# A hybrid GLA and NSA decoder trunk on one core: off-diagonal probability blocks of two head groups in fp32

## The chip, the cores and the metric

The kernel runs on one NeuronCore of a Trainium2 chip. The metric is the device time of one execution in microseconds; what is compared is the median of several runs. The core has five engines that matter here: TensorE (PE in the profile, its weight loads are PEld), VectorE (DVE), ScalarE (ACT), GpSimd (POOL) and SyncE (SP), which issues DMAs.

## The reference

The kernel computes two layers on 512 tokens of 1024 channels: a gated linear attention (GLA) and a native sparse attention (NSA), each followed by a mixture of 16 experts, with a layer norm behind every part. The change lies in the NSA. With 512 tokens in blocks of 64 there are 8 blocks and the selection takes up to 16, so all causal blocks are selected, and the window of 512 reaches back over all tokens. What remains are three causal softmax attentions per head, mixed by sigmoid gates:

```python
p_cmp = masked_softmax(einsum(q, k_cmp), cmask);  o_cmp = p_cmp @ v_cmp
p_slc = masked_softmax(einsum(q, k_sel), smask);  o_slc = p_slc @ v_sel
p_win = masked_softmax(einsum(q, k_win), wmask);  o_win = p_win @ v_win
o = gate0 * o_cmp + gate1 * o_slc + gate2 * o_win
```

There are 16 heads in 4 groups; a group shares keys and values.

## The kernel before

Most products are made of fp16 halves: a value is split into a high part (a cast) and a low part (the value less the high part), and high x high, high x low and low x high are accumulated.

The attention is `nsa_attn` (line 1405). Its unit of work is (t, g, b): token tile t of 128 queries, head group g of 4 heads, and branch b (0 selected, 1 window). `order` (lines 1507 and 1508) has 32 units: i = 0 to 7 are tile 3, i = 8 to 15 tile 2 (for g = 0: i = 8 and 9, for g = 1: i = 10 and 11), i = 16 to 23 tile 1, i = 24 to 31 tile 0. `begin(i + 2)` starts the scores of a unit two units ahead of its `pv`.

`scores` (1443) goes over the key tiles j from t down to 0. Two matmuls of 512 columns make a bank of transposed scores for four heads (1448, 1449); the exponential (1452) reads it. A block whose `exact` is set has its exponential written as fp32 into the tile `ph`; that holds for the diagonal block j == t of tiles 2, 1 and 0 (1450), which GpSimd masks (1455). Any other block has it written into a buffer `pf`, of which there are three, and `split` (1411) makes the halves in `ph`. Which engine makes the high half goes by a running count through `HI_BY = 'daeeee'`: d is a VectorE cast, a a ScalarE copy, e a second exponential on ScalarE straight from the bank (where the block was masked, a copy). The low half is a subtraction on VectorE, or, for tile 3 alone, at times on GpSimd.

`pv` (1461) multiplies, per head: for a diagonal block of tiles 2 to 0 one fp32 product with `VF`, the fp32 copy of V (1469), for any other block three narrow fp16 products with the halves of V (1472 to 1474). `V` and `VF` carry a column of ones, so the sum for the softmax comes with the 64 values: 65 columns. `combine` (1489) takes the reciprocal of that sum, multiplies by the gate, and adds into the row `o` (1493 to 1505). `cmp_pv` (1477) does the compressed branch with matmuls on 32 rows (1483 to 1486).

There are eight PSUM banks for all of it. The attention is interleaved with other work: the output projection's weight units are split in i = 5, 6, 8 and 11 (`whl` from `wha`, lines 178 and 180); behind tile 3's last unit come its transposes (273), and from i = 11 its output projection (256 to 258). The order of the instructions on an engine is set when the program is built, by dependence and by their order in the source; an engine then works through its own queue in order.

Of the kernel before, what the change touches and what calls it, by code (L numbers as in the profile page):

```python
# [9 lines left out]
F32 = mybir.dt.float32  # L10
# [11 lines left out]
NT = 4  # L22
# [20 lines left out]
OTT = 1  # L43
REST_AT = (0, 2, 3, 4)
CMP_AT = 4
SPLIT_AT = (5, 6, 8, 11)
SPLIT_BY = 'dddd'
WCH = 4
# [11 lines left out]
class Trunk:  # L60
# [1344 lines left out]
    def nsa_attn(self, T, pool, early, rest, kcA, kcB, vc, kA, kB, V, VF, qA, qB, gate):  # L1405
        nc = self.nc
# [4 lines left out]
        def split(hi, lo, src, ps=None, share=False):  # L1411
            i = cnt[0]
            cnt[0] += 1
            how = HI_BY[i % len(HI_BY)]
            if how == "e" and ps is not None:
                self.exp_ins = nc.scalar.activation(hi, ps, AF.Exp)
            elif how in "ea":
                nc.scalar.activation(hi, src, AF.Copy)
            else:
                nc.vector.tensor_copy(hi, src)  # L1420
            if share and ps is not None and LO_BY[i % len(LO_BY)] == "p":
                nc.gpsimd.tensor_sub(lo, src, hi)
            else:
                nc.vector.tensor_sub(lo, src, hi)

        def cmp_scores(t):
            cs = self.bank()
            nc.tensor.matmul(cs.rearrange("p (h q) -> p h q", h=4), self.identb,
                             self.cmt[:, t][:, None, :].to_broadcast([P, 4, P]), start=True, stop=False,
                             skip_group_check=True)  # L1430
            for g in range(4):
                gs = slice(g * 32, (g + 1) * 32)
                nc.tensor.matmul(cs[gs], kcA[:, gs], qa(g, t), start=False, stop=False, skip_group_check=True,
                                 tile_position=(0, g * 32))
                nc.tensor.matmul(cs[gs], kcB[:70, gs], qb(g, t), start=False, stop=(g == 3), skip_group_check=True,
                                 tile_position=(0, g * 32))
            pc = T([P, S], "pf", F32, 3)
            nc.scalar.activation(pc, cs, AF.Exp)
            pch = T([P, 2, S], "pch", F16, 2)
            split(pch[:, 0], pch[:, 1], pc)  # L1440
            return pch

        def scores(t, g, b):
            ph = self.wp.tile([P, 4, 2, S], F16, name="ph", tag="wst", bufs=NST)
            for j in range(t, -1, -1):
                st = self.bank()
                js = slice(j * P, (j + 1) * P)
                nc.tensor.matmul(st, kA[b][:, g, js], qa(g, t), start=True, stop=False)
                nc.tensor.matmul(st, kB[b][:70, g, js], qb(g, t), start=False, stop=True)
                exact = j == t < NT - 1  # L1450
                pf = ph[:, j].rearrange("p i q -> p (i q)").bitcast(F32) if exact else T([P, S], "pf", F32, 3)
                self.exp_ins = nc.scalar.activation(pf, st, AF.Exp)
                if j == t:
                    v = pf.rearrange("p (h q) -> p h q", h=4)
                    nc.gpsimd.affine_select(v, v, pattern=[[0, 4], [1, P]], compare_op=OP.is_ge, fill=0.0,
                                            base=0, channel_multiplier=-1)
                if not exact:
                    split(ph[:, j, 0], ph[:, j, 1], pf, None if j == t else st, t == NT - 1)
            return ph

        def pv(t, g, b, ph):
            ob = self.bank()
            for h in range(4):
                hs = slice(h * P, (h + 1) * P)
                o0 = ob[:, h * 65:(h + 1) * 65]
                exact = t < NT - 1
                if exact:
                    pf = ph[:, t].rearrange("p i q -> p (i q)").bitcast(F32)
                    nc.tensor.matmul(o0, pf[:, hs], VF[b][t][:, g], start=True, stop=(t == 0))
                last = t if exact else t + 1  # L1470
                for j in range(last):
                    nc.tensor.matmul(o0, ph[:, j, 0, hs], V[b][j][:, g, 0:65], start=(j == 0 and not exact), stop=False)
                    nc.tensor.matmul(o0[:, :64], ph[:, j, 0, hs], V[b][j][:, g, 65:129], start=False, stop=False)
                    nc.tensor.matmul(o0, ph[:, j, 1, hs], V[b][j][:, g, 0:65], start=False, stop=(j == last - 1))
            return ob

        def cmp_pv(g, pch):
# [31 lines left out]
        pch, o, ph = {}, {}, {}  # L1509

        def begin(i):
            if i < len(order):
                t, g, b = order[i]
                if g == 0 and b == 0:
                    if t < 3:
                        pch[t] = cmp_scores(t)
                    o[t] = self.row("o")
                ph[i] = scores(t, g, b)
# [4 lines left out]
        for i, (t, g, b) in enumerate(order):  # L1523
# [5 lines left out]
            if t < 3 and b == 0:  # L1529
                combine(t, g, 0, cmp_pv(g, pch[t]), o[t], True)  # L1530
            combine(t, g, 1 + b, pv(t, g, b, ph.pop(i)), o[t], t == 3 and b == 0)
            self.pump()
            if i == REST_AT[-1]:
# [7 lines left out]
                units = [self.fetch_aside(u) for u in range(3)]  # L1541
            if i in SPLIT_AT:
                by = SPLIT_BY[SPLIT_AT.index(i)]
                self.op[0].append(self.split(units.pop(0), (), nc.gpsimd if by == "p" else None))
                if i == SPLIT_AT[0]:
                    units.append(self.fetch_aside(3))
            if i == CMP_AT:
                pch[3] = cmp_scores(3)
# [133 lines left out]
```

## Time and profile before

| | us |
|---|---|
| median of three runs (954.68 to 956.17) | 954.74 |
| profiled execution | 952.24 |
| its span, first to last instruction | 950.5 |
| TensorE busy | 877.9 |
| VectorE busy | 744.7 |
| ScalarE busy | 555.7 |
| GpSimd busy | 310.8 |

The attention takes the stretch from about 575 to 725 us of the span. In the rows below a line gives the start or the stretch first, then a duration; L1472 is line 1472 of the kernel, `bank<-V,ph` what is written and read, a bracket behind it the idle time of the engine just before it and what ended it. TensorE's matmuls overlap, so the pace of a run of them is read from start to start.

### The profile page before, as it was taken

What the parts mean: (1) busy time and instruction counts of PE and PEld (TensorE: products, weight loads), DVE (VectorE), ACT (ScalarE), POOL (GpSimd) and SP (SyncE); (2) the same over time, 40 slices, a digit from 0 to 9 for tenths busy, and PEclk for the clock granted to TensorE, in tenths of its full rate; (3) what the DMA queues carried; (4) which work ended last, traced back from release to release, by engine and by line L of the source; (5) the groups of instructions that cost most, each with busy time, mean ns of one, the idle gap of its engine ahead of it and who ended that gap; (6) DMA issues with size and microseconds to landing.
All of it is one profiled execution on the core that took longest, in us unless ns stands there. A gap on an engine that the chain in (4) does not pass through costs nothing. (4 is left out here: it accounts for less than half of the span.)

```text
span 950.5 us, 26582 instructions
## 1 busy us (share of the span) xinstructions
PE 877.9 (92%) x11218; PEld 718.4 (76%) x11218; DVE 744.7 (78%) x1666; ACT 555.7 (58%) x1174; POOL 310.8 (33%) x349
## 2 busy tenths in 40 slices
PE   6999999996799999899989998999999669999994
PEld 2468888876698989668978885767888568888871
DVE  5972225889899999798678765689777899999967
ACT  4823324424499999724644437784544449999940
POOL 0210021003435241530254524543430348623153
PEclk9999999998899999999999999979999879999997
DMA  8662322072399998871322001120005549999683
GB/s 294 247 205 84 128 90 89 1 300 86 114 374 408 377 378 314 212 205 46 134 89 90 1 3 45 52 85 1 2 2 225 219 180 384 404 369 378 238 156 111
DMA packets 29278, 169.19 MB, mean 178 GB/s; under 512 B 3521, under 2 KB 4161, under 8 KB 12641
## 3 DMA queue, kind: packets, MB, share of 16 engines
q1 hardware_dynamic: 23168, 144.49, 40.0%
q0 software_dynamic: 3072, 12.72, 6.0%
q10 hardware_dynamic: 2912, 10.23, 2.8%
q8 instruction: 90, 1.47, 0.6%
q14 instruction: 36, 0.29, 0.1%
HBM read 153.91 MB, written 13.50 MB: 176 GB/s over the span
## 5 line engine op out<-in xcount | busy, mean ns | idle before, releaser
L834 POOL TENSOR_SCALAR ohe<-icap,rt_px 128x96 f16<-128x96 f32 x112 | 114.1, 1033 | 132.8 <-PE bank L923 124.4
L180 DVE SCALAR_TENSOR_TENSOR whl<-wsu,whl 128x512 f16<-128x512 f32 x192 | 127.2, 714 | 2.9 <-ACT whl L178 2.8
L180 DVE SCALAR_TENSOR_TENSOR whl<-wst,whl 128x512 f16<-128x512 f32 x116 | 75.5, 702 | 67.4 <-ACT whl L178 67.4
L178 ACT ACTIVATE whl<-wsu 128x512 f16<-128x512 f32 x192 | 106.7, 624 | 3.2 <-PE bank L258 3.2
L845 PE MATMUL bank<-ohe,xs 128*128 128x96 f16 x2048 | 99.1, 212 | 6.6 <-DVE ohe L834 5.5
L178 ACT ACTIVATE whl<-wst 128x512 f16<-128x512 f32 x144 | 80.8, 624 | 33.1 <-PE bank L249 9.8
L845 PEld LDWEIGHTS <-xs 128*128 128x128 f16 x2048 | 94.5, 101 | 7.2 <-DVE ohe L834 4.5
L180 DVE SCALAR_TENSOR_TENSOR wha<-wst,wha 128x512 f16<-128x512 f32 x144 | 94.1, 705 | 3.1 <-ACT wha L178 3.0
L258 PE MATMUL bank<-whl,xt 128*128 128x256 f16 x320 | 87.1, 273 | 1.0 <-DVE xt L232 1.0
L256 PE MATMUL bank<-whl,xt 128*128 128x256 f16 x320 | 87.2, 273 | 0.8 <-ACT xt L231 0.7
L257 PE MATMUL bank<-whl,xt 128*128 128x256 f16 x320 | 87.2, 273 | 0.0
L178 ACT ACTIVATE wha<-wst 128x512 f16<-128x512 f32 x144 | 79.8, 623 | 3.4 <-DMA wst<-moe 3.2
L920 PE MATMUL bank<-xh,whl 128*128 128x96 f16 x576 | 75.2, 207 | 0.0
L918 PE MATMUL bank<-xh,whl 128*128 128x96 f16 x576 | 75.2, 207 | 0.0
L919 PE MATMUL bank<-xh,whl 128*128 128x96 f16 x576 | 75.2, 207 | 0.0
L258 PE MATMUL bank<-whl,oT 128*128 128x256 f16 x256 | 69.7, 273 | 1.6 <-DVE oT L232 1.6
L256 PE MATMUL bank<-whl,oT 128*128 128x256 f16 x256 | 69.8, 273 | 0.5 <-ACT oT L231 0.5
L258 PE MATMUL bank<-whl,xT 128*128 128x256 f16 x256 | 69.8, 273 | 0.0
L257 PE MATMUL bank<-whl,xT 128*128 128x256 f16 x256 | 69.8, 273 | 0.0
L256 PE MATMUL bank<-whl,xT 128*128 128x256 f16 x256 | 69.8, 273 | 0.0
L257 PE MATMUL bank<-whl,oT 128*128 128x256 f16 x256 | 69.8, 273 | 0.0
L919 PE MATMUL bank<-xh,wha 128*128 128x96 f16 x448 | 61.3, 210 | 0.8 <-PEq L986 0.8
(405 smaller groups left out, 2751.9 us busy)
## 6 DMA issues: line engine op xcount, KB each, us to landing
wsu<-moe SPq DMA_DIRECT2D x54, 1024.0 KB, 8.2
wst<-moe SPq DMA_DIRECT2D x42, 1024.0 KB, 7.8
wst<-gla_in SPq DMA_DIRECT2D x11, 1024.0 KB, 4.8
yslots<-y ACTq DMA_DIRECT2D x26, 384.0 KB, 7.0
wst<-nsa_in SPq DMA_DIRECT2D x9, 1024.0 KB, 4.9
wst<-gla_out SPq DMA_DIRECT2D x4, 1024.0 KB, 4.7
wha<-nsa_out SPq DMA_DIRECT2D x4, 1024.0 KB, 4.8
xs<-xT SPq DMA_DIRECT2D x4, 512.0 KB, 6.8
```

The source lines that it names most:

```text
L178: self.hi_ins = nc.scalar.activation(hl[:, 0, s], st[:, s], AF.Copy, scale=WS)
L180: nc.vector.scalar_tensor_tensor(hl[:, 1, s], st[:, s], WS, hl[:, 0, s], op0=OP.mult, op1=OP.subtract)
L256: nc.tensor.matmul(out, xt[0][:, k], w[0][:, s], start=(k == 0), stop=False)
L257: nc.tensor.matmul(out, xt[0][:, k], w[1][:, s], start=False, stop=False)
L258: nc.tensor.matmul(out, xt[1][:, k], w[0][:, s], start=False, stop=(k == KT - 1))
L834: eng.tensor_scalar(part[e][0][:, t], self.icap, self.px[:, t, e:e + 1], None, op0=OP.is_equal)
L845: nc.tensor.matmul(banks[half][:, j * CAP:(j + 1) * CAP], xs[t][:, i, k * P:(k + 1) * P], oh[:, t], start=(j == 0 and t == self.order[0] a ...
L918: nc.tensor.matmul(o, w[0][:, s], xh[:, 0, k], start=(k == 0), stop=False)
L919: nc.tensor.matmul(o, w[1][:, s], xh[:, 0, k], start=False, stop=False)
L920: nc.tensor.matmul(o, w[0][:, s], xh[:, 1, k], start=False, stop=(k == KT - 1))
```

## The change

A tuple `WHOLE` names two pairs of token tile and head group, (2, 0) and (2, 1). For these, in both branches, all the blocks of a unit are exact: the exponential is written as fp32 into `ph`, no halves are made, and `pv` multiplies the fp32 block with `VF`. For all other units the blocks are treated as before. In `pv` the exact blocks come first, then the others. Since `split` runs less often, the count that picks the engine from `HI_BY` is eight lower for every later block.

```diff
--- before.py
+++ after.py
@@ -43,6 +43,7 @@
 OTT = 1
 REST_AT = (0, 2, 3, 4)
 CMP_AT = 4
+WHOLE = (2, 0), (2, 1)
 SPLIT_AT = (5, 6, 8, 11)
 SPLIT_BY = 'dddd'
 WCH = 4
@@ -1440,6 +1441,9 @@
             split(pch[:, 0], pch[:, 1], pc)
             return pch
 
+        def whole(t, g):
+            return [] if t == NT - 1 else list(range(t, -1, -1)) if (t, g) in WHOLE else [t]
+
         def scores(t, g, b):
             ph = self.wp.tile([P, 4, 2, S], F16, name="ph", tag="wst", bufs=NST)
             for j in range(t, -1, -1):
@@ -1447,7 +1451,7 @@
                 js = slice(j * P, (j + 1) * P)
                 nc.tensor.matmul(st, kA[b][:, g, js], qa(g, t), start=True, stop=False)
                 nc.tensor.matmul(st, kB[b][:70, g, js], qb(g, t), start=False, stop=True)
-                exact = j == t < NT - 1
+                exact = j in whole(t, g)
                 pf = ph[:, j].rearrange("p i q -> p (i q)").bitcast(F32) if exact else T([P, S], "pf", F32, 3)
                 self.exp_ins = nc.scalar.activation(pf, st, AF.Exp)
                 if j == t:
@@ -1463,15 +1467,17 @@
             for h in range(4):
                 hs = slice(h * P, (h + 1) * P)
                 o0 = ob[:, h * 65:(h + 1) * 65]
-                exact = t < NT - 1
-                if exact:
-                    pf = ph[:, t].rearrange("p i q -> p (i q)").bitcast(F32)
-                    nc.tensor.matmul(o0, pf[:, hs], VF[b][t][:, g], start=True, stop=(t == 0))
-                last = t if exact else t + 1
-                for j in range(last):
-                    nc.tensor.matmul(o0, ph[:, j, 0, hs], V[b][j][:, g, 0:65], start=(j == 0 and not exact), stop=False)
+                exact = whole(t, g)
+                blocks = exact + [j for j in range(t + 1) if j not in exact]
+                for j in blocks:
+                    start, stop = j == blocks[0], j == blocks[-1]
+                    if j in exact:
+                        pf = ph[:, j].rearrange("p i q -> p (i q)").bitcast(F32)
+                        nc.tensor.matmul(o0, pf[:, hs], VF[b][j][:, g], start=start, stop=stop)
+                        continue
+                    nc.tensor.matmul(o0, ph[:, j, 0, hs], V[b][j][:, g, 0:65], start=start, stop=False)
                     nc.tensor.matmul(o0[:, :64], ph[:, j, 0, hs], V[b][j][:, g, 65:129], start=False, stop=False)
-                    nc.tensor.matmul(o0, ph[:, j, 1, hs], V[b][j][:, g, 0:65], start=False, stop=(j == last - 1))
+                    nc.tensor.matmul(o0, ph[:, j, 1, hs], V[b][j][:, g, 0:65], start=False, stop=stop)
             return ob
 
         def cmp_pv(g, pch):
```

## Rows read from the trace of the kernel before

**Rows 1.** the page: span, and the TensorE clock granted in 40 slices.

```profile
span 950.5 us, 26582 instructions
...
PEclk9999999998899999999999999979999879999997
```

**Rows 2.** by stretch: length; busy us (count) of PE, PEld, DVE, ACT, POOL; clock, DMA.

```profile
623.70:626.40 2.70, 1.69 (x44) 1.29 (x40) 2.60 (x8) 2.70 (x7) 0.00 (x0) 1.00 0.40 61
626.40:636.60 10.20, 9.56 (x67) 6.16 (x68) 10.20 (x26) 8.35 (x17) 4.85 (x6) 0.50 0.21 88
636.60:647.50 10.90, 10.07 (x131) 7.65 (x130) 9.80 (x24) 8.15 (x17) 5.64 (x8) 1.00 0.01 2
...
657.90:725.00 67.10, 66.60 (x782) 54.46 (x779) 50.16 (x164) 30.05 (x56) 21.47 (x30) 1.00 0.03 8
```

**Rows 3.** TensorE in order of time, token tile 0: sixteen fp32 records; columns: start, us, instruction.

```profile
722.73 2.00 PE L1469 MATMUL bank<-VF,ph 128*128 128x65 f32 x16
724.56 0.27 PE L256 MATMUL bank<-whl,oT 128*128 128x256 f16 x1
```

**Rows 4.** the same view, token tile 3: first of 48 narrow fp16 matmuls, and the next.

```profile
615.82 0.20 PE L1472 MATMUL bank<-V,ph 128*128 128x65 f16 x1
...
617.29 0.38 PE L1428 MATMUL bank<-cmt,identb 128*128 128x512 bf16 x1
```

**Rows 5.** the same view from 623 to 632, three waits (in brackets) and the first pv.

```profile
623.83 0.20 PE L1483 MATMUL bank<-vc,pch 32*128 32x65 f16 x1
...
625.31 0.18 PE L1483 MATMUL bank<-vc,pch 32*128 32x65 f16 x1 [0.45 <-ACT ph L1416]
...
626.40 0.23 PE L1483 MATMUL bank<-vc,pch 32*128 32x65 f16 x1 [0.56 <-DVE ott L1504]
...
627.87 0.59 PE L1448 MATMUL bank<-qA,kA 128*128 128x512 f16 x1 [0.64 <-ACT ph L1452]
...
630.52 0.23 PE L1483 MATMUL bank<-vc,pch 32*128 32x65 f16 x1
...
631.29 0.69 PE L1469 MATMUL bank<-VF,ph 128*128 128x65 f32 x2
631.77 0.26 PE L1472 MATMUL bank<-V,ph 128*128 128x65 f16 x1
```

**Rows 6.** the same view from 634 to 648: later units of token tile 2 and the projection.

```profile
634.55 0.62 PE L1448 MATMUL bank<-qA,kA 128*128 128x512 f16 x1
...
638.54 0.85 PE L273 MATMUL bank<-identf,o 128*128 128x128 f32 x6
639.88 0.44 PE L273 MATMUL bank<-identf,o 128*128 128x128 f32 x2 [0.49 <-POOL o L1505]
640.15 0.38 PE L1448 MATMUL bank<-qA,kA 128*128 128x512 f16 x1
...
643.78 0.38 PE L1448 MATMUL bank<-qA,kA 128*128 128x512 f16 x1
...
645.15 0.38 PE L1448 MATMUL bank<-qA,kA 128*128 128x512 f16 x1 [0.34 <-ACT pf L1452]
...
647.50 0.27 PE L256 MATMUL bank<-whl,oT 128*128 128x256 f16 x1
```

**Rows 7.** ScalarE in order of time, the splits of the first unit of token tile 2.

```profile
624.62 0.65 ACT L1416 ACTIVATE ph<-bank 128x512 f16<-128x512 f32 x1
625.09 2.24 ACT L178 ACTIVATE whl<-wha 128x512 f16<-128x512 f32 x4
627.17 0.65 ACT L1452 ACTIVATE ph<-bank 128x512 f32<-128x512 f32 x1
```

**Rows 8.** VectorE in order of time, the same units.

```profile
624.99 0.17 DVE L1495 RECIPROCAL ocf<-bank 128x4 f32<-128x4 f32 x1
625.08 0.66 DVE L1424 TENSOR_TENSOR ph<-pf,ph 128x512 f16<-128x512 f32 x1
...
625.91 0.43 DVE L1504 TENSOR_TENSOR ott<-bank,ocf 128x256 f32<-128x256 f32 x1
```

## The prediction

> **What bounds the kernel now.** I read the views from the coarse to the fine. The page gives the span, and the granted clock in 40 slices [rows 1]: a dip falls into the slice that holds 630 us, in the middle of the attention, where the edit lies. The busy time by stretch comes next [rows 2]. From 657.9 to 725 TensorE is busy 66.60 of 67.10 us, so what it does before that point sets when everything behind it begins; VectorE is as full only from 623.7 to about 637 (10.20 of 10.20 us in the third stretch) and ScalarE is never full after 626.4. The reader is to see a second thing there: from 626.4 to 636.6 the granted clock is 0.50, the 1.2 GHz level, while TensorE counts as busy 9.56 of 10.20 us. Then I read TensorE in order of time. Before the fall it came out of a dense run of fp16 matmuls at 623.8, did narrow matmuls on 32 of the 128 rows, and stood waiting for a bank between them: 0.45 us until ScalarE's second read of a score bank, 0.56 us until VectorE's product, 0.64 us until an exponential [rows 5]. Before the rise at 636.6 it did six score matmuls of 512 columns, from 634.55 [rows 6]. So in these 24 us (623.8 to 647.5) three things add up: TensorE's own work, waits on late ScalarE and VectorE, and half-speed work. The edit touches all three.
>
> **The change part by part.**
>
> *TensorE.* Two head groups by two branches are four units (i = 8 to 11). Each has two off-diagonal blocks and four heads: 32 times, three fp16 matmuls give way to one fp32 product. 48 fp16 ones take 617.29 - 615.82 = 1.47 us, so 0.031 each and 0.092 for three [rows 4]. Sixteen fp32 records are eight products (each is recorded twice); they take 724.56 - 722.73 = 1.83 us, 0.229 each [rows 3]. The difference is 0.137 us, times 8 is 1.10 us per unit, times 4 is 4.4 us, all on TensorE, all at the full clock. At the low level one fp32 product takes 631.77 - 631.29 = 0.48 us [rows 5].
>
> The Trainium skill, page "FP8 and Floating Point Precision", section "TensorE Precision Notes", has true fp32 as four passes through the array. By that rule four passes of 0.031 would make 0.124 us and the edit would cost 32 x 0.031 = 1.0 us and not 4.4, as an estimate. The trace shows 0.229 us for this very instruction, so the measurement decides and no chance hangs on the rule.
>
> *ScalarE and VectorE.* Eight splits go. By the cycle of `HI_BY` the eight high halves are seven on ScalarE (six of them second exponentials out of the bank) and one cast on VectorE; the eight low halves are all VectorE. One ScalarE read costs 625.09 - 624.62 = 0.47 us of its queue [rows 7], seven 3.3 us. One subtraction costs the time to the next start, 0.57 to 0.66 us [rows 8], eight about 5 us; the one cast I leave out of the sum. Most of that is worth nothing by itself, since TensorE sets the pace; worth is what shortens its waits. In unit 8 both second reads go: the four weight splits at 625.09 start 0.95 us sooner, and the exponential at 627.17, for which the score matmul at 627.87 waits, ends near 626.85 [rows 5, 7]. The wait of 0.45 us goes with the read that caused it. On VectorE the subtraction at 625.08 goes from between the reciprocal and the product at 625.91; the product starts at about 625.4 and the last narrow run near 625.9 instead of 626.40 [rows 5, 8]. So the scores of unit 10 start at 626.9, 1.0 us sooner than 627.87. If ScalarE's order changes as well so that nothing is late there, they start after two more narrow runs, at about 625.8. I take 626.9, because it needs no new order.
>
> *What is moved.* The exponential writes fp32 into the tile that the halves used, so three-deep `pf` buffers are not taken for eight blocks; that can only free ScalarE. The cycle of `HI_BY` continues eight places earlier: some later blocks of tiles 2 and 1 change engine. I cost it at nothing: TensorE covers it (66.60 of 67.10 us [rows 2]). Without that cover a block that changes engine puts at most one more read of 0.47 us into a queue [rows 7]. No DMA is added, no wait is added: the products need the exponential alone, or the mask on GpSimd for the diagonal as before.
>
> *The sum, with the full clock held.* A unit with its narrow run takes 643.78 - 640.15 = 3.63 us; the narrow run in it is about 0.39 (half of 631.29 - 630.52 at the low level [rows 5]), so a unit without it takes 3.24 [rows 6]. With 1.10 added these are 4.73 and 4.34. The transposes take 640.15 - 638.54 = 1.61 us less their wait of 0.49, which goes because VectorE is ahead, so 1.12 [rows 6]. 626.9 + 4.73 + 4.34 + 1.12 + 4.73 + 4.34 = 646.2; the projection began at 647.50. That is 1.3 us sooner; with some of the small wait of 0.34 us at 645.15 gone in its surroundings too I take 1.4. The profiled execution took 952.24 us, 1.74 more than its span; 1.4 less is 950.8. The median of the runs shown, 954.74, lies 2.5 us above the profiled one, so the forecast for a median is 953.3. Bounds of this case: 2.5 sooner with the start at 625.8, 3.7 with VectorE's 5 us reaching the last weight splits; 0.7 later than now if a new order of instructions costs what the earlier start gave.
>
> **The rivals.**
>
> *The low clock stays until the projection.* The place is 623.8 to 626.9: the dense run, the four narrow runs and two of the waits are still there, only 1.0 us shorter, so what went before the fall is mostly unchanged. What ended it, in the present trace, was a stretch with fp16 pv and 512-column scores. After the edit each pv is twelve fp32 products instead of four and 24 fp16 ones, and at the low level 12 x 0.48 = 5.8 us stand between one unit's scores and the next. The low level held through fp32 products before although TensorE counted as busy nearly all the time [rows 2, 5]. It decides if the clock falls at all and the scores alone don't lift it. Price: scores 630.52 - 627.87 = 2.65 four times, narrow runs 0.77 twice, pv 5.8 four times, transposes 2.2: 37.5 us from 626.9 make 664.4, which is 16.9 late. The projection's own start is slow until the clock rises; the last rise came 2.1 us into the scores, so 1 to 2 us more. Some 18 us: 972.7, bounds 971 to 974. For it: the row of the fall. Against it: 1.0 us less of the thin stretch, and that the scores of unit 10 come that much sooner.
>
> By the Trainium skill, page "TensorE: Matmul & The Clock Gate", Part 1, the low level is the default and activity lifts it. The trace agrees that it is not the busy share of the page that counts: 9.56 of 10.20 us busy, and low throughout.
>
> *The low clock ends after one or two units*, as now. To the end of unit 9's scores: 626.9 + 2.65 + 0.77 + 5.8 + 2.65 = 638.8, then at the full clock pv 2.9, transposes 1.1, and two units 4.73 and 4.34 give 651.9, which is 4.4 late: 959.1. A unit or two more at the low level adds 4 each: up to 968.
>
> *The gain is swallowed.* VectorE and ScalarE get nothing but idle time and the projection's weight halves or the expert weights' transfers set the later start: then 954 to 955. TensorE's 66.60 of 67.10 us speaks against it.
>
> **How the numbers follow.** Full clock held: 0.58. Low to the projection: 0.21. Low for a part: 0.17. Swallowed: 0.04. About 0.2%, 1.9 us, is what a measurement of this kernel can tell from no change: 952.8 to 956.6. The first case lies at its edge, with its own range from 951.0 to 955.4; I split it 0.34 faster, 0.24 same. The fourth goes to same: 0.28. The two low cases are slower: 0.38. The predicted time is 953.3. The range runs from 951.0 over the second rival up to the middle of the first, 972.5; it leaves out half of the first and the tail of the forecast, under 2 in 10.
>
> **What would show it.** The fp32 records of the attention rise from 192 to 256, and the narrow fp16 ones fall by 32 on each of three lines. If the fp32 price is right, a pv of units 8 to 11 takes 2.9 us at the full clock. If the waits go as said, the scores of unit 10 start near 626.9 with no wait on a second read. The granted clock between 626 and 664 decides among the cases: full and the projection at 646, or low and at 652 to 664. The prediction is wrong if the clock is held and the projection still begins later than 648, or if it begins sooner and the end does not follow.

## The result and the profile after

The changed kernel is slower: a median of 964.64 us in five runs (964.04 to 965.60) against 954.74 us for the kernel before in the same comparison, a recorded ratio of 1.0114 with a 95% interval of 1.0092 to 1.0136. (The quotient of these two medians is 1.0104; it lies in the interval.) The profiled execution took 964.04 us with a span of 962.0, against 952.24 and 950.5 [rows 1].

The page of after: the span and TensorE's granted clock in 40 slices, and the busy time of the engines.

```profile
span 962.0 us, 26493 instructions
...
PE 887.1 (92%) x11186; PEld 726.6 (76%) x11186; DVE 737.9 (77%) x1657; ACT 551.9 (57%) x1167; POOL 300.0 (31%) x349
...
PEclk9999999998899999999999999959999889999997
```

VectorE and ScalarE have 6.8 and 3.8 us less to do, as the change says, and TensorE counts 9.2 us more. In the clock's row the dip at 630 us has gone from 7 to 5: the low stretch lasts longer. By stretch, with the columns of [rows 2]:

```profile
624.70:627.30 2.60, 1.56 (x54) 1.38 (x50) 2.46 (x7) 2.60 (x7) 0.35 (x1) 1.00 0.34 57
627.30:647.90 20.60, 19.05 (x89) 14.77 (x86) 13.08 (x41) 10.09 (x20) 8.76 (x11) 0.50 0.11 45
647.90:656.00 8.10, 8.10 (x72) 6.75 (x71) 5.59 (x15) 4.76 (x9) 2.58 (x4) 1.00 0.01 2
```

The granted clock fell to 0.50 (1.2 GHz) at 627.3, 0.9 us later than before, and stayed there for some 20.5 us, where it was 10.2 [rows 2]. TensorE counts as busy for 19.05 of 20.60 us of it. The same engine in order of time, with the columns of [rows 3]:

```profile
624.81 0.20 PE L1489 MATMUL bank<-vc,pch 32*128 32x65 f16 x1
...
626.93 0.20 PE L1489 MATMUL bank<-vc,pch 32*128 32x65 f16 x1 [1.04 <-DVE ott L1510]
...
627.88 0.59 PE L1452 MATMUL bank<-qA,kA 128*128 128x512 f16 x1 [0.41 <-ACT ph L1456]
...
631.12 0.23 PE L1489 MATMUL bank<-vc,pch 32*128 32x65 f16 x1 [0.52 <-DVE ott L1510]
...
632.57 0.87 PE L1476 MATMUL bank<-VF,ph 128*128 128x65 f32 x3 [0.61 <-DVE ocf L1499]
...
637.71 0.63 PE L1452 MATMUL bank<-qA,kA 128*128 128x512 f16 x1
...
640.27 5.22 PE L1476 MATMUL bank<-VF,ph 128*128 128x65 f32 x24
645.29 1.91 PE L274 MATMUL bank<-identf,o 128*128 128x128 f32 x8
646.99 0.63 PE L1452 MATMUL bank<-qA,kA 128*128 128x512 f16 x1
...
649.29 2.89 PE L1476 MATMUL bank<-VF,ph 128*128 128x65 f32 x24
652.02 0.38 PE L1452 MATMUL bank<-qA,kA 128*128 128x512 f16 x1
...
653.33 2.79 PE L1476 MATMUL bank<-VF,ph 128*128 128x65 f32 x24
655.95 0.27 PE L257 MATMUL bank<-whl,oT 128*128 128x256 f16 x1
```

Four things are to be seen. The narrow run behind the dense one begins at 624.81, 1.0 us later than in [rows 5]: this execution was already that much behind ahead of any changed instruction (the narrow matmuls of [rows 4] begin at 616.80 instead of 615.82). Counted from the start of the narrow run the clock fell at the same place as before: 627.3 - 624.81 = 2.5 us behind it, where it was 626.4 - 623.83 = 2.6. From the start of the narrow run to the scores of unit 10 it takes 627.88 - 624.81 = 3.07 us, where it took 4.04; the wait on the second read has gone, but VectorE's product is still waited for, for 1.04 us, and two new waits on VectorE follow, 0.52 and 0.61. The pv of units 8 and 9, all fp32, run at the low clock, 637.71 - 632.57 = 5.14 and 645.29 - 640.27 = 5.02 us long; those of units 10 and 11 at the full clock take 652.02 - 649.29 = 2.73 and 655.95 - 653.33 = 2.62. In the kernel before the pv of units 10 and 11 began at these lines and took 643.78 - 642.02 = 1.76 and 647.50 - 645.74 = 1.76 us [rows 6]:

```profile
642.02 0.44 PE L1469 MATMUL bank<-VF,ph 128*128 128x65 f32 x2
...
645.74 0.44 PE L1469 MATMUL bank<-VF,ph 128*128 128x65 f32 x2
```

Last, the projection begins at 655.95, where it began at 647.50 [rows 6]: 8.45 us late, 7.5 without the 1.0 from upstream.

These 7.5 us can be added up, as an estimate from the rows: the low stretch is 10.3 us longer at half speed, 5.1; four units with about 0.95 more at the full clock, 3.8; the thin stretch 1.0 shorter. That makes 7.9, 0.4 too much.

From the projection to the end another 3 us are lost. One row of after and the one of before that answers to it, both from TensorE in order of time, show 0.8 of it:

```profile
742.09 0.28 PE L259 MATMUL bank<-whl,oT 128*128 128x256 f16 x1 [1.89 <-DVE oT L233]
```

```profile
732.54 0.28 PE L258 MATMUL bank<-whl,oT 128*128 128x256 f16 x1 [1.06 <-DVE oT L232]
```

The last projection waits 1.89 us for VectorE's copy instead of 1.06. This goes with the fp32 products and not with the new count for `HI_BY`: of the runs below, `cycle` and `price`, which have the products and the old count, wait 1.89 us there, and `relief`, which has neither the products nor the old count, waits 1.06. The rest is spread over the experts, and no row holds it.

### The profile page after: what moved, and what is told of

Its sections match the earlier page's. It is cut to its first block, busy times and chain, and to the rows that moved or that the text cites. A ratio compares the mean times of both kernels' runs of the same rounds, so it can differ in the third digit from the quotient of the medians.

```text
span 962.0 us, 26493 instructions
## 1 busy us (share of the span) xinstructions
PE 887.1 (92%) x11186; PEld 726.6 (76%) x11186; DVE 737.9 (77%) x1657; ACT 551.9 (57%) x1167; POOL 300.0 (31%) x349
## 5 line engine op out<-in xcount | busy, mean ns | idle before, releaser
L835 POOL TENSOR_SCALAR ohe<-icap,rt_px 128x96 f16<-128x96 f32 x112 | 104.2, 945 | 144.1 <-PE bank L924 136.9
```

The costliest lines, as they stand in the source:

```text
L835: eng.tensor_scalar(part[e][0][:, t], self.icap, self.px[:, t, e:e + 1], None, op0=OP.is_equal)
```

## The experiments

Two theories stood after the traces were read. Mine, A in the expectations: the fp32 products are the cause, by their own length and by the clock that stays low while they run in units 8 and 9, and the work taken from ScalarE and VectorE is worth next to nothing. Against it stand rivals that have the loss in something that came along (the new count for `HI_BY`, the earlier or later fall of the clock, the thin stretch ahead of it, or simply more TensorE time between two units' scores, whatever the products); each expectation says which it means.

One execution's low stretches vary, the unchanged kernel's too. So each run is also read by its mean granted clock c: (1 - c) x 2 x span is the time at the low level. In the profiled runs that sum agrees with the low stretches of the trace to within some 3 us. The time less half of it is an estimate of what the kernel would take at the full clock throughout, as if all of the low time were TensorE's at half speed. Half is a high price: over the 70 runs of before a line through time and low time rises by 0.35 us per us at the low level, so the last column takes off too much where the low time is long.

Means over the runs, in us. "Before" is the 70 runs of the four comparisons of the experiments. The five of the comparison above have no clock on record and are not in it; their mean is 955.0, so there after is 9.8 us slower, and 11.2 against the 70.

| kernel | runs | median | ratio, 95% interval | mean | at the low clock | mean less half of it |
|---|---|---|---|---|---|---|
| before | 70 | 954.0 | | 953.5 | 62.3 | 922.4 |
| after | 5 | 964.64 | 1.0114 (1.0092 to 1.0136) | 964.7 | 73.5 | 928.0 |
| relief | 10 | 954.3 | 1.0009 (0.9989 to 1.0029) | 954.4 | 65.3 | 921.7 |
| price | 4 | 963.39 | 1.0134 (1.0060 to 1.0208) | 964.9 | 74.7 | 927.6 |
| late | 10 | 958.32 | 1.0056 (1.0035 to 1.0078) | 958.9 | 61.1 | 928.4 |
| one_group | 7 | 962.47 | 1.0079 (1.0048 to 1.0110) | 961.1 | 75.6 | 923.3 |
| dense | 10 | 956.16 | 1.0037 (1.0015 to 1.0058) | 956.7 | 62.7 | 925.4 |
| cycle | 5 | 962.8 | 1.0108 (1.0067 to 1.0149) | 963.3 | 73.1 | 926.7 |
| spread | 6 | 962.63 | 1.0088 (1.0058 to 1.0119) | 962.6 | 66.6 | 929.3 |
| spread_before | 10 | 957.78 | 1.0040 (1.0019 to 1.0060) | 958.0 | 69.0 | 923.5 |
| fill | 4 | 965.16 | 1.0115 (1.0071 to 1.0158) | 964.4 | 65.0 | 931.9 |
| fill_before | 10 | 957.45 | 1.0041 (1.0021 to 1.0061) | 957.6 | 60.4 | 927.4 |
| resplit | 4 | 961.86 | 1.0110 (1.0056 to 1.0165) | 962.5 | 72.5 | 926.2 |
| resplit_before | 10 | 953.65 | 0.9995 (0.9972 to 1.0017) | 953.0 | 62.2 | 921.9 |

### Both halves of the change alone: relief and price

`relief` is the kernel before without the splits of the change's eight off-diagonal blocks: the exponential writes fp16 once, and three fp16 products are still made from it. `price` is the changed kernel with the splits put back into buffers that nobody reads, so that TensorE's new products stand and the other engines get no relief.

```diff
# relief, against before
...
+                if j != t and (t, g) in WHOLE:
+                    self.exp_ins = nc.scalar.activation(ph[:, j, 0], st, AF.Exp)
+                    continue
...
# price, against after
+                if exact and j != t:
+                    sc = T([P, S], "pf", F32, 3).bitcast(F16).rearrange("p (i q) -> p i q", i=2)
+                    split(sc[:, 0], sc[:, 1], pf, st, False)
```

> The kernel before, but for the off-diagonal blocks of the two head groups no halves are split: one exponential writes fp16, and the third narrow product repeats the second's operands, so the low part of the probabilities is left out and the low part of V counts twice. ScalarE and VectorE do about as little as in the changed kernel, TensorE does the narrow fp16 products of before. Theory A (the fp32 products cost 4.4 us and, at the low clock, keep the clock low): the low stretch is as long as before, 10.2 us or less, the scores of unit 10 start about 1 us sooner, 952 to 954.5. Theory B (the longer low stretch comes from the shifted work of ScalarE and VectorE): low for about 20 us, 958 to 961.

> The changed kernel, but the halves of those blocks are still split, into a buffer that nothing reads: the work of ScalarE and VectorE of before with the fp32 products of the change. Theory A: low for 20 us or more, 965 to 970. Theory B: low for about 10 us, 958 to 960 (the 4.4 us of the products alone).

`relief` took 954.3 us, a ratio of 1.0009 whose interval holds 1; `price` 963.39, below the range expected and about as slow as after, though its four runs lie far apart (959.90 to 972.96). In `relief` the count for `HI_BY` has moved as in the change, and in `price` it has not. So all of the loss is with the products, and the relief is worth nothing that can be measured, though it is what the forecast's gain was made of. The low stretch by the rows of both (columns of [rows 2]), `relief` first:

```profile
625.80:642.90 17.10, 15.60 (x100) 11.10 (x100) 14.08 (x40) 10.15 (x20) 8.85 (x11) 0.50 0.13 54
```

```profile
625.50:646.00 20.50, 19.86 (x95) 15.43 (x96) 18.21 (x46) 11.49 (x23) 8.61 (x10) 0.50 0.11 44
```

In `price` it is 20.5 us as in after. In `relief` the clock fell as well, and in this one execution it was low for 17.1 us, where I expected 10.2 or less. Over its ten runs the low time is 65.3, 3 above before's. That the clock falls thus does not hang on the fp32 products; and relieving the two engines did not keep it up.

### The same products where the clock is full: late

```diff
-WHOLE = (2, 0), (2, 1)
+WHOLE = (2, 2), (2, 3)
```

> The changed kernel with the pair (2, 2), (2, 3) instead: units 12 to 15, behind the place where the clock was low before. Theory A (about 4 us from the fp32 products at the full clock, about 5 us from a longer low stretch, to which fp32 products at the low clock add): the low stretch is that of before, 957 to 959. Theory C (the products and what waits on them are the whole loss, wherever they stand): 963 to 966.

The same number of fp32 products, in units 12 to 15. Measured: 958.32 us. The low stretch, and two of the fp32 pv in TensorE's order of time, then the same two units in the kernel before:

```profile
627.20:637.40 10.20, 9.53 (x67) 6.14 (x68) 10.20 (x26) 8.36 (x17) 4.82 (x6) 0.50 0.22 90
```

```profile
660.68 2.89 PE L1476 MATMUL bank<-VF,ph 128*128 128x65 f32 x24
663.41 0.38 PE L1452 MATMUL bank<-qA,kA 128*128 128x512 f16 x1
...
664.72 2.79 PE L1476 MATMUL bank<-VF,ph 128*128 128x65 f32 x24
667.34 0.38 PE L1429 MATMUL bank<-cmt,identb 128*128 128x512 bf16 x1
```

```profile
659.85 0.44 PE L1469 MATMUL bank<-VF,ph 128*128 128x65 f32 x2
...
661.60 0.38 PE L1448 MATMUL bank<-qA,kA 128*128 128x512 f16 x1
...
662.91 0.33 PE L1469 MATMUL bank<-VF,ph 128*128 128x65 f32 x2
...
664.57 0.38 PE L1428 MATMUL bank<-cmt,identb 128*128 128x512 bf16 x1
```

The low stretch is the 10.2 us of before. The two pv take 663.41 - 660.68 = 2.73 and 667.34 - 664.72 = 2.62 us, where they took 1.75 and 1.66 before: 0.96 to 0.98 more per unit, 3.9 for four. The projection of tile 2 that follows began 4.8 us late (686.62 instead of 681.80), 0.8 of it from upstream. So this is the price of the products without that of the clock: some 4 us on TensorE, 5 in the mean of the time. After pays 6 more for the same number of products, and its low time is 12.4 us longer, which at half speed is 6.2, and 4.3 at 0.35 per us. Theory C of the expectations, the same loss wherever the products stand, had 963 to 966.

### Half of the products: one_group

```diff
-WHOLE = (2, 0), (2, 1)
+WHOLE = (2, 0),
```

> The changed kernel with the pair (2, 0) alone: units 8 and 9, the two that run at the low clock. Theory A: half of the fp32 products, 2 us, and most of the longer low stretch, since both units stand in it: 958 to 961. Theory C (loss in proportion to the products): 959, half of 11 us; told apart by the low stretch in the trace, 17 us or more by A, 10 to 14 by C.

If the loss went with the number of products, half would be left. Measured: 962.47, above the range of either theory, and in the mean 7.6 of after's 11.2 us, two thirds. The low stretch:

```profile
628.00:648.50 20.50, 18.90 (x83) 14.61 (x82) 14.47 (x43) 9.51 (x19) 8.12 (x10) 0.50 0.06 23
```

It is as long as in after, 20.5 us, and the low time of all seven runs is 75.6, while the time without half of it is only 0.9 above before's. Units 8 and 9 alone are enough for the longer low stretch. Units 10 and 11 make 3.6 us of the mean (964.7 - 961.1); their length at the full clock is 1.8 of that, and the rest isn't settled.

### More TensorE work of another kind in the same units: dense

The kernel before with 32 more narrow fp16 products in each of units 8 to 11, overwritten by what follows. TensorE is given about as much more to do as by the change, and nothing else is touched.

```diff
+                if t == 2 and g < 2:
+                    for n in range(8):
+                        nc.tensor.matmul(o0, ph[:, n % 2, 0, hs], V[b][n % 2][:, g, 0:65], start=True, stop=True)
```

> The kernel before, but each pv of units 8 to 11 has eight more narrow fp16 products per head ahead of it, whose result is overwritten: 32 x 0.031 = 1.0 us more per unit at the full clock, as much as the fp32 products cost in a unit of the same size (0.96 us). TensorE is busy as long as in the changed kernel, but with dense narrow products. Theory A (it is the fp32 products that keep the clock low): low time as before, 60 to 66 us over the span, 957 to 959.5. Theory D (it is the longer pv between two units' scores, of whatever kind): low time 72 us or more, 962 to 966.

Measured: 956.16 us, 0.8 us below the range of theory A, and 62.7 us at the low clock, that of before. In the profiled execution the clock was low for 6.8 us:

```profile
630.90:637.70 6.80, 6.80 (x72) 5.15 (x70) 6.80 (x20) 5.65 (x13) 2.58 (x4) 0.50 0.07 25
```

So here more time between two units' scores didn't keep the clock low when narrow fp16 products filled it. In after, `price`, `one_group` and `cycle`, with fp32 products of the same 65 columns, the low time is 73 to 76 us. An fp32 product differs from the fp16 ones in its weight loads too; no run parts the two.

### The count for the engines: cycle

```diff
+                if exact and j != t:
+                    cnt[0] += 1
```

> The changed kernel, but the count behind HI_BY goes on by one for each block that is no longer split, so that every later block keeps the engine that it had before. If the shifted cycle is part of the loss: 1 us or more less than the changed kernel, 961 to 963.5. If TensorE covers it, as forecast: 964 to 965.5.

With it every later block goes to the engine that it had before. The median is 962.8, in the range expected if the count is part of the loss; the mean is 1.5 us below after's, and the intervals overlap by far. Five runs each don't settle it. But `price` has the old count too and a mean of 964.9, and `relief` has the new one and loses nothing that can be measured, so no run needs the count as a cause.

### Three ways to keep the clock from falling, on both kernels

The reason that I gave for the fall was the thin stretch from 623.8 on: a narrow run on 32 rows with waits in it. Each of these edits takes something from it. `spread` puts the four compressed products of unit 7 one by one into units 5 to 8:

```diff
-            if i == 7:
-                for h in range(4):
-                    combine(3, h, 0, cmp_pv(h, pch[3]), o[3], False)
+            if 5 <= i <= 8:
+                combine(3, i - 5, 0, cmp_pv(i - 5, pch[3]), o[3], False)
```

> The changed kernel with tile 3's four narrow runs of the compressed branch spread over i = 5 to 8 instead of all at i = 7, so that TensorE has no thin stretch before unit 10. Theory A: the clock stays full between 620 and 660, the projection begins about 10 us sooner, 952 to 956. Theory C (the fp32 products and what waits on them are the whole loss, the clock only goes with it): 961 to 965.

> The kernel before with the same spreading. Theory A: no low stretch at 626, about 5 us less, 948.5 to 951. Theory C: 954 to 955.5, as before.

Both missed theory A: 962.63, in the range of theory C, and 957.78, above both. The fall only moved, to 633.6 with the change and to 631.5 without it, and the low stretch lasted 17.1 us in both. The row with the change:

```profile
633.60:650.70 17.10, 16.47 (x76) 13.76 (x77) 9.62 (x31) 5.99 (x12) 5.23 (x7) 0.50 0.01 1
```

Where it moved to there is a new wait, by the waits of TensorE in `spread` (line waited for; us in total, times, longest):

```profile
PE bank L1476 <- DVE ocf L1499: 2.4, 1, 2.4
```

The pv of unit 8 waits 2.4 us for VectorE; in `spread_before` it waits 2.6 for another product of the same engine.

`fill` keeps the order and puts three matmuls of 512 columns ahead of each narrow run of unit 7, into the bank that it then overwrites:

```diff
...
+            for _ in range(fill):
+                nc.tensor.matmul(ob, kA[1][:, g, 0:P], qa(g, 2), start=True, stop=True)
...
-                    combine(3, h, 0, cmp_pv(h, pch[3]), o[3], False)
+                    combine(3, h, 0, cmp_pv(h, pch[3], 3), o[3], False)
```

> The changed kernel with three more matmuls of 512 columns ahead of each of tile 3's four narrow runs; what they write is overwritten. They fill the thin stretch before unit 10 and cost TensorE 12 x 0.22 = 2.6 us, of which 1.4 lie in waits. Theory A: no low clock between 620 and 660, or a short one; 955 to 959 in spite of the added work. Theory C: 965 to 967.

> The kernel before with the same twelve added matmuls. Theory A: no low clock there, 949 to 952. Theory C: 954.5 to 957, the added work.

With the change TensorE waited 1.3 us for VectorE ahead of unit 8's pv (635.88 to 639.49). The clock was full up to the middle of that pv and fell at 637.6, for 13.7 us:

```profile
637.60:651.30 13.70, 13.70 (x55) 10.35 (x53) 9.47 (x26) 4.16 (x8) 6.85 (x8) 0.50 0.00 1
```

The low time is 8.5 us less than after's, but the time is after's: 965.16. The added matmuls and their waits cost about as much as the clock gave; on the kernel before they cost 4.1 us of the mean at about the same low time (957.45). Both missed theory A. The row has one more thing: TensorE counts as busy for all of 13.70 us, and the clock is low.

`resplit` moves the second and third set of weight splits from units 6 and 8 to units 8 and 9, so that ScalarE's exponentials come sooner:

```diff
-SPLIT_AT = (5, 6, 8, 11)
+SPLIT_AT = (5, 8, 9, 11)
```

> The changed kernel with the output projection's second weight unit split at i = 8 and the third at i = 9 instead of i = 6 and i = 8: ScalarE and VectorE are free of four passes of 0.5 and 0.8 us just where unit 10's scores wait. Theory A: unit 10's scores start 2 us sooner, the clock is low for less than 10 us or not at all between 620 and 660, 955 to 960. Theory C: 962 to 965.

> The kernel before with the same order of weight splits. Theory A: no low clock, or less than 7 us, at 626: 949 to 952. Theory C: 953 to 956.

The thin stretch became shorter still: the scores of unit 10 began 2.3 us after the dense run's end (622.92 to 625.25). The clock fell all the same:

```profile
626.30:643.40 17.10, 16.27 (x77) 13.72 (x76) 10.61 (x37) 8.68 (x18) 7.42 (x8) 0.50 0.09 36
```

961.86 us with the change, just below theory C and a miss of theory A. Without it 953.65, a ratio of 0.9995: no gain either, with a stretch of 10.2 us at the low clock. These three edits were each made on both kernels, so the price of the change can be read three more times:

| | mean, change less before | low time, change less before |
|---|---|---|
| as it is | 11.2 | 11.2 |
| with `resplit` | 9.5 | 10.3 |
| with `fill` | 6.8 | 4.6 |
| with `spread` | 4.6 | -2.4 |

The change costs more where it brings more low time. With `spread` it brings none: the low stretch is 17.1 us with and without the fp32 products, and the loss is about that of `late`. So the products don't lengthen the low stretch wherever they meet it, and the part of the loss that isn't clock is there each time, some 4 to 7 us with the low time priced at 0.35 to 0.5 per us. No version that beats the kernel before was found.

## Why the prediction was wrong

The step that failed is "the sum, with the full clock held", to which the prediction gave 0.58. It was reasoned from a thin stretch that would be 1.0 us shorter. That stretch did become 1.0 us shorter, and the clock fell all the same, 2.5 us behind its start instead of 2.6, and was low for some 20.5 us, where the sum has none; in `resplit` it was 2.3 us instead of 4.04 in length, and the clock fell too. The shorter stretch was thus no ground for a held clock. All of the forecast gain hung on it: the prediction's own terms, 4.4 us for the products less 1.0 for the earlier start and 0.5 for the transposes' wait, make a loss of some 3 us if the low stretch only stays as it was. The range held the measured time because it was drawn over the rivals. In the trace of every kernel run here the clock fell somewhere between 625 and 638. What remains open is what exactly makes it fall; three guesses at that didn't hold.

Point by point:

- *The price of the products*: a unit was to cost 1.10 us more and cost about 0.95 (0.86 and 0.97 in after, 0.96 and 0.98 in `late`). The fp32 side was right, 2.73 / 12 = 0.228 a product against 0.229 [rows 3]. What was mis-sized is what goes: 0.092 for three fp16 products came from a long run of them [rows 4]. Among fp32 products they were slower: a pv of units 10 and 11 took 1.76 in the trace of before; less four fp32 products, 0.92, this leaves 0.84 for eight triples, 0.105 each. At the low level a product took 5.14 / 12 = 0.43 and not 0.48, which came from a single one [rows 5].
- *The relief*: right in its place and size, 3.07 us instead of 4.04 to the scores of unit 10, and without value. `relief` has it without the products, and is no faster. The gain was to come through TensorE's earlier start; behind it stand new waits on VectorE, 0.52 and 0.61 in after and 0.51 and 0.61 in `relief`, and the low clock.
- *The shift of `HI_BY`* at nothing: not refuted; `cycle` would allow some 1.5 us, `price` none, and `relief`, which moves the count too, loses nothing.
- *The end follows the projection*: not quite. 8.45 us there became 11.5 at the end of the span. `late` has the same, 4.8 at its projection and 6 at the end, so 3 us in after and 1 in `late` come behind that projection, 0.8 and 0.5 of it in the longer wait of the last one (1.89 and 1.53 instead of 1.06). What makes the rest isn't settled.
- *The rivals*: "the low clock ends after one or two units" is what happened, with its chance of 0.17. Its text has the projection at 651.9 and 4 us more for a unit more at the low level, 655.9. (What it calls unit 9's scores in that sum are those of unit 11.) The second pv and the transposes ran at the low level as well, and the projection began at 655.95. That the two agree so closely is in part luck, since 1.0 us of the measured lateness is from upstream. The time that this gives, 963.1, is 1.5 below the median measured. "Low to the projection" was too pessimistic: the level rose at 647.9, in the stretch with the transposes (645.29) and the scores of unit 12 (646.99), before the pv of units 10 and 11. The prediction's sentence that the trace agrees on the busy share says more than its rows do: they show only that the profile's busy share didn't tell the level.
- *The change does what it says*: 256 fp32 records instead of 192, and 32 fewer narrow ones on each of three lines.

So of the mean's 11.2 us some 4 to 6 are the longer low time (73.5 - 62.3 = 11.2 us: 3.9 at 0.35 per us, 5.6 at half speed; `late`, with the same products and no longer low stretch, is 5.8 faster than after), and 5 to 7 the rest, 3.7 to 4 of it the products' own length.

## What to carry to other kernels

Ahead of an edit near a stretch at the low clock, price every rival at that level, and count what the edit puts into it: here products that cost 0.95 us more per unit at the full clock cost about twice that there (the pv of unit 8 took 5.14 us instead of 634.55 - 631.29 = 3.26 [rows 5, 6]), and the level stayed low for 10 us more. An earlier start is no reason for a held clock, and work taken from engines other than the one that sets the pace is worth nothing until a run shows it. One experiment that moves the same work to a stretch at the full clock parts the length from the clock.

## What the runs showed of the hardware

TensorE's busy share in the profile didn't tell the level of its clock: in after 19.05 of 20.60 us and in `fill` 13.70 of 13.70 were busy and low. Rows of narrow fp32 products (65 columns) went by at the low level without a rise, 24 records in 5.22 us. In the traces of kernels whose pv in these units has only four fp32 products the low stretch was 6.8 us (`dense`, `fill_before`), 10.2 (before, `late`, `resplit_before`) and 17.1 (`relief`, `spread_before`); with twelve it was 13.7 (`fill`), 17.1 (`spread`, `resplit`) and 20.5 (after, `price`, `one_group`, `cycle`). The two overlap, so the means over the runs, and not a single trace, carry the reading.

The start-to-start time of the narrow fp32 products is that of two weight loads. TensorE's weight loads in `late`, in order of time:

```profile
660.67 2.75 PEld L1476 LDWEIGHTS bank<-VF,ph 128*128 128x128 f32 x24
```

24 loads, two for each of twelve products, fill 2.75 us, 0.114 each; the twelve products take 2.73. The exchange of three fp16 products for one fp32 product saves a third of the loads and loses time all the same: fp16 products with their loads start every 0.031 us [rows 4]. That the loads are what holds the products up fits this and isn't shown by a run of its own.

One kernel's low time isn't the same in every execution: the 70 runs of before lie between 53 and 69 us, and their times follow it, with a mean of 955.1 at a mean clock near 0.965 (37 runs) and of 951.4 near 0.9705 (25 runs). By the Trainium skill, page "TensorE: Matmul & The Clock Gate", Part 1, the point at which the level changes differs between runs of the same kernel. The spread of the low time fits that; no run here shows the point itself in two executions of one kernel. A difference of a few microseconds between two single profiled executions can be no more than that.
